# Second layer's expert stage: 56 rows ahead instead of 42, 14 of them parked in DRAM, eight rows' gates kept on chip, and gate products tied to the low half of W two rows back

## The chip, the cores and the metric

The kernel runs on one core of a Trainium2 chip. The metric is the time of one execution on the device in microseconds, as the median of three runs. One further execution was taken by the hardware profiler; all rows below come from it.

## The reference, cut to what matters

The reference is a two-layer block over 256 context tokens and 256 latent tokens of width 1024. Each layer has a mixer (a gated unit, a state space scan and gated linear attention) and then a feed-forward part that picks experts by product keys. The change lies in that second part:

```python
def block(xb):                                   # 128 tokens
    q = (xb @ w_query).reshape(128, 8, 2, 128)
    s = jnp.einsum('thpd,phkd->thpk', q, keys)   # 8 heads, two lists of 128 keys
    s1, i1 = lax.top_k(s[:, :, 0], 16);  s2, i2 = lax.top_k(s[:, :, 1], 16)
    cand = s1[..., :, None] + s2[..., None, :]   # 256 candidate pairs per head
    top_s, pos = lax.top_k(cand, 16)             # 16 experts of 128*128 per head
    gate = jax.nn.softmax(top_s, axis=-1)
    act = gelu(einsum('td,thkd->thk', xb, expert_u[idx]))
    return einsum('thk,thkd->td', gate * act, expert_v[idx])
```

The second layer gives out latent tokens only, so it works on two blocks of 128 tokens; the first layer works on four (one of them by gathering experts).

## The kernel before, in words

For most token blocks the kernel does not gather experts. It computes all 128 x 128 of them, row by row: row `e` holds the 128 experts whose first key is `e`. `U(e)` (lines 1324 to 1344) streams one 512 KB tile of expert_u, splits it into a high and a low half (`split`, lines 69 to 72: ScalarE casts `uhi`, VectorE subtracts `ulo`), has TensorE make the activations in `pu` (24 matrix products for two blocks, `mm3`, line 77) and lets ScalarE apply gelu into a tile that waits for its turn. `V(e)` (lines 1351 to 1375) streams a tile of expert_v, splits it in the same way (`vhi`, `vlo`), has VectorE multiply the activations by the gates (line 1362, "the gate product" below), splits the result into the two halves of W (`whl`: ScalarE casts the high one, line 1364, VectorE subtracts the low one, line 1365) and has TensorE add 12 products of 512 columns to the sums `acc` (line 1374).

The gates come from `gates`. For each group of 32 tokens VectorE builds one-hot matrices (`oh2`, `oh1l`, `oh1h`, `oh2s`, lines 1219 to 1227), TensorE multiplies them into `gps` (lines 1232, 1233), ScalarE copies them to `gst`, and a 2 MB write on ScalarE's queue stores them in DRAM (`gd`, line 1237). GpSimd copies the gates of rows 0 to 3 to `gt0` (line 1236); the gates of later rows are read back from DRAM four rows at a time into `gt` (line 1356), which has two buffers. In the second layer there are 8 groups and one `gt` is 512 KB.

The V rows need the gates, and the gates of all tokens. Until these are there TensorE works on U rows ahead of time: `LEAD` rows of them, 42 in the second layer. 16 of the 42 activations lie in four row buffers, the rest in `act` tiles. In the first layer `SPILL` rows are parked: their gelu goes to `aout` (two buffers), is written to DRAM on ScalarE's queue (line 1344) and read back into `ain` (three buffers, line 1349) two rows ahead of its use. After the rows ahead V rows run alone until U has to follow, and then U and V alternate, with U four rows ahead at the least (`KEEP`).

The order of the instructions on each engine is not the program's. A scheduler sets it when the kernel is built, from a timeline that it simulates; an engine then takes its instructions strictly in that order, so one that waits holds up all behind it on that engine. `self.after(...)` (line 55) makes the instructions that are traced inside it come behind a given one on the same engine. SyncE's queue issues all loads of `eraw` (five buffers), `gt` and `ain`, also in order.

Of the kernel before, what the change touches and what calls it, by code (L numbers as in the profile page):

```python
# [10 lines left out]
F32 = mybir.dt.float32  # L11
# [5 lines left out]
OP = mybir.AluOpType  # L17
# [11 lines left out]
PLAN = {"s5": ((4, 1, 0, 0, 0, 0), (4, 0, 0, 0, 0, 0)), "gla": ((1, 1, 1, 1, 0, 1, 1), (2, 2, 1, 1, 0, 1))}  # L29
DEPTH = 2  # L30
NI1 = 128
LEAD = {0: 40, 1: 42}
KEEP = 4
TOGETHER = {0: 4, 1: 3}
SPILL = {0: 22, 1: 0}
AHEAD = 2
ERAW = 5
GPS = 3
# [11 lines left out]
class Kernel:  # L50
# [1129 lines left out]
                self.topk_head(b, h, s, p)  # L1180


    def gates(self, l, blocks, p, ps):

        nc = self.nc
        gd = self.dp.tile([4 * len(blocks), 128, NI1 * 32], F32, name=f"gd{l}", bufs=1)
        sels = {}
        with self.pool(f"selx{l}", side="right") as sp:
            es = {b: self.pick_exp(b, sp, len(blocks)) for b in blocks}
            for b in blocks:  # L1190
                w = self.pick(b, sp, es[b])
                tb = ps.tile([128, 3, 128], F32, name="selp", tag="gps", bufs=GPS)
                for z in range(3):
                    nc.tensor.transpose(tb[:, z], w[:, z], self.ident)

                sels[b] = self.selp.tile([128, 4, 128, 2], F16, name=f"sel{b}", bufs=1)
                g = sp.tile([128, 2, 128], F32, name="gsel", bufs=2)
                nc.scalar.copy(sels[b][:, 0:2], tb[:, 0:2, :, None].to_broadcast([128, 2, 128, 2]))
                nc.scalar.mul(g[:, 0], tb[:, 2], 2.0 ** 14)
                nc.vector.tensor_copy(sels[b][:, 2], g[:, 0, :, None].to_broadcast([128, 128, 2]))  # L1200
                nc.vector.tensor_tensor(g[:, 1], g[:, 0], sels[b][:, 2, :, 0], op=OP.subtract)
                nc.vector.tensor_scalar(sels[b][:, 3], g[:, 1, :, None].to_broadcast([128, 128, 2]), 2.0 ** 12, None,
                                        op0=OP.mult)
        self.es_tv.close()

        self.gt0 = self.selp.tile([128, 4 * len(blocks), 4, 32], F32, name="gt0")
        with self.pool(f"gate{l}", side="right") as p:
            for k, b in enumerate(blocks):
                sel = sels[b]
                for tg in range(4):  # L1210
                    st = p.tile([128, NI1, 32], F32, name="gst", bufs=2)
                    for q in range(32 // OHT):
                        t = 32 * tg + OHT * q
                        ts = (128, OHT, 64, 2)
                        io = self.iota.rearrange("p (a b) -> p a b", b=2)[:, None].to_broadcast(ts)
                        at = lambda z: sel[:, z, t:t + OHT][:, :, None].to_broadcast(ts)
                        one = lambda nm: p.tile([128, OHT, 64, 2], F16, name=nm, bufs=OHB)
                        o2, o2s, oh, ol = one("oh2"), one("oh2s"), one("oh1h"), one("oh1l")
                        nc.vector.tensor_tensor(o2, io, at(1), op=OP.is_equal)
                        e = OSC[q % len(OSC)]  # L1220
                        if e == "a":
                            nc.scalar.mul(o2s, o2, 2.0 ** -12)
                        else:
                            nc.vector.tensor_scalar(o2s, o2, 2.0 ** -12, None, op0=OP.mult)
                        nc.vector.tensor_tensor(ol, io, at(0), op=OP.is_equal)
                        nc.vector.tensor_tensor(oh, ol, at(2), op=OP.mult)
                        nc.vector.tensor_tensor(ol, ol, at(3), op=OP.mult)
                        flat = lambda a, z: a[:, z].rearrange("p a b -> p (a b)")
                        for z0 in range(0, OHT, 4):
                            pb = ps.tile([128, 4, 128], F32, name="gps", tag="gps", bufs=GPS)  # L1230
                            for z in range(4):
                                nc.tensor.matmul(pb[:, z, :], flat(o2, z0 + z), flat(oh, z0 + z), start=True, stop=False)  # L1232
                                nc.tensor.matmul(pb[:, z, :], flat(o2s, z0 + z), flat(ol, z0 + z), start=False, stop=True)  # L1233
                            o = OHT * q + z0
                            nc.scalar.mul(st[:, :, o:o + 4], pb.rearrange("p t i -> p i t"), 2.0 ** -14)
                    nc.gpsimd.tensor_copy(self.gt0[:, 4 * k + tg], st[:, 0:4, :])
                    nc.scalar.dma_start(gd[4 * k + tg], st.rearrange("p i t -> p (i t)"))
        return gd

# [53 lines left out]
    def peer(self, l, dense):  # L1293
        nc, i = self.nc, self.i
# [5 lines left out]
        with ExitStack() as es:  # L1300
            p = es.enter_context(self.pool(f"peer{l}"))
            acts_a = es.enter_context(self.pool(f"acta{l}"))
            es_b = es.enter_context(ExitStack())
            acts_b = es_b.enter_context(self.pool(f"actb{l}"))
            lead, spill = LEAD[l], SPILL[l]
            per, away = 1024 // nt, {}
            pu_ = es.enter_context(self.pool(f"psu{l}", space=PSUM))
            with self.pool(f"psg{l}", space=PSUM) as gp:
                gd = self.gates(l, dense, p, gp)
            pa = es.enter_context(self.pool(f"psa{l}", space=PSUM))  # L1310
            p2 = es.enter_context(self.pool(f"peerv{l}", side="right"))
            acc = [[pa.tile([128, 512], F32, name=f"acc{b}{h}", bufs=1) for h in range(2)] for b in range(nb)]
            acts, gt, rows, todo, left = {}, {}, {}, [], []

            def stream(src, nm):
                raw = p.tile([128, 1024], F32, name="eraw", bufs=ERAW)
# [7 lines left out]
            def U(e):  # L1324
# [10 lines left out]
                elif e < 4 * per + spill:  # L1335
                    acts[e] = p.tile([128, nt], F32, name="aout", bufs=2)
                elif e < lead - KEEP:
                    acts[e] = acts_b.tile([128, nt], F32, name="act", bufs=lead - KEEP - 4 * per - spill)
                else:
# [9 lines left out]
                    nc.sync.dma_start(acts[e], away[e])  # L1349

            def V(e):
                if e == 0:
                    gt[0] = self.gt0
                elif e % 4 == 0:
                    gt[0] = p2.tile([128, 4 * nb, 4, 32], F32, name="gt", bufs=2)
                    nc.sync.dma_start(gt[0].rearrange("p g a b -> p g (a b)"),
                                      gd.rearrange("g p x -> p g x")[:, :, 32 * e:32 * e + 128])
# [1 line left out]
                hi, lo = stream(i["v"][l, e], "u" if late < TOGETHER[l] and late % 2 else "v")  # L1359
                a = acts.pop(e)  # L1360
                av = a.rearrange("p (g t) -> p g t", t=32)
                nc.vector.tensor_tensor(av, av, gt[0][:, :, e % 4, :], op=OP.mult)
                w = p2.tile([128, 2, nt], F32R, name="whl", bufs=max(3, TOGETHER[l]))
                nc.scalar.copy(w[:, 0], a)  # L1364
                self.v_lo = nc.vector.tensor_tensor(w[:, 1], a, w[:, 0].bitcast(F32), op=OP.subtract)
                todo.append((e, hi, lo, w))
                if 0 < late < TOGETHER[l]:
                    return
# [69 lines left out]
            for k, b in enumerate(sorted(out)):  # L1438
# [3 lines left out]
                st = ep.tile([128, 2], F32, name="fst", bufs=2) if last else self.xst[:, b]  # L1442
# [10 lines left out]
                else:  # L1453
                    nc.vector.tensor_tensor(st[:, 0:1], st[:, 0:1], st[:, 1:2], op=OP.add)
                    self.rstd(st[:, 1:2], st[:, 0:1], 1024)
                    if k == 0:
                        fg = ep.tile([128, 1024], F32, name="fg", bufs=1)
                        f = i["final_g"]
# [122 lines left out]
```

## Time and profile before

| | us |
|---|---|
| median of three runs | 2751.05 |
| lowest, highest | 2743.09, 2753.84 |
| profiled execution | 2751.38 |
| its span, first to last instruction | 2749.6 |
| TensorE busy | 2627.0 (96%) |
| VectorE busy | 2037.9 (74%) |
| ScalarE busy | 1188.9 (43%) |
| GpSimd busy | 430.6 (16%) |

The span holds both layers one after the other; the second layer's U rows begin near 1930 us, its gates end near 2116 us. TensorE's busy time counts pipelined products, so its rate is better read from how far apart products start. The 1.8 us between the span and the execution's time lie around it.

### The profile page before, as it was taken

What the parts mean: (1) busy time and instruction counts of PE and PEld (TensorE: products, weight loads), DVE (VectorE), ACT (ScalarE), POOL (GpSimd) and SP (SyncE); (2) the same over time, 40 slices, a digit from 0 to 9 for tenths busy, and PEclk for the clock granted to TensorE, in tenths of its full rate; (3) what the DMA queues carried; (4) which work ended last, traced back from release to release, by engine and by line L of the source; (5) the groups of instructions that cost most, each with busy time, mean ns of one, the idle gap of its engine ahead of it and who ended that gap; (6) DMA issues with size and microseconds to landing.
All of it is one profiled execution on the core that took longest, in us unless ns stands there. A gap on an engine that the chain in (4) does not pass through costs nothing.

```text
span 2749.6 us, 44156 instructions
## 1 busy us (share of the span) xinstructions
PE 2627.0 (96%) x16911; PEld 2272.0 (83%) x16911; DVE 2037.9 (74%) x4342; ACT 1188.9 (43%) x1808; POOL 430.6 (16%) x342
## 2 busy tenths in 40 slices
PE   7899999999899999999999999998897999999998
PEld 4777888899678899988899977768796789999997
DVE  8755589899788988988978755558998655555554
ACT  3353334566234333333333333524475454444443
POOL 0001000021023443434534200010011000000000
PEclk9998999999999999999999999989998999999999
DMA  7521423577689999999999837444566766666663
GB/s 275 135 86 63 169 84 116 203 292 290 207 282 330 335 332 344 326 333 345 327 343 334 319 119 203 135 158 165 184 242 249 252 211 211 207 207 208 211 210 115
DMA packets 250035, 629.59 MB, mean 229 GB/s; under 512 B 25376, under 2 KB 117856, under 8 KB 247008
## 3 DMA queue, kind: packets, MB, share of 16 engines
q1 hardware_dynamic: 197072, 432.41, 47.0%
q0 software_dynamic: 36864, 134.23, 13.6%
q10 hardware_dynamic: 15888, 60.14, 6.1%
q8 instruction: 132, 2.16, 0.3%
q14 instruction: 79, 0.65, 0.1%
HBM read 566.04 MB, written 59.61 MB: 228 GB/s over the span
## 4 chain that ended last, share of the span: by engine, by line
PE 82%; DVE 11%; DMA 3%; issue 2%; ACT 1%; POOL 0%; SPq 0%; POOLq 0%; DVEq 0%; ACTq 0%
PE pu L77 32%; PE acc L1374 31%; PE prT L275 6%; PE prN L288 3%; PE opp L941 1%; PE modp L157 1%; DMA mraw<-in_w_mod_dram 1%; PE gps L1233 1%; PE gps L1232 1%; DMA gt<-gd 1%; PE yp L633 1%; DVE wlo L72 1%; DVE ulo L72 1%; DVE ti L1092 1%; DVE s L1090 1%
## 5 line engine op out<-in xcount | busy, mean ns | idle before, releaser
L1374 PE MATMUL acc<-vhi,whl 128*128 128x512 f32 x2528 | 726.9, 398 | 3.2 <-ACT whl L1364 3.2
L77 PE MATMUL pu<-hTh,uhi 128*128 128x384 f32 (+1 forms) x2048 | 604.2, 313 | 11.3 <-ACT s L1176 7.5
L77 PE MATMUL pu<-hTl,uhi 128*128 128x384 f32 (+1 forms) x2048 | 603.0, 313 | 0.0
L1374 PEld LDWEIGHTS acc<-vhi,whl 128*128 128x128 f32 x2528 | 471.5, 190 | 107.1 <-ACT whl L1364 3.5
L72 DVE TENSOR_TENSOR vlo<-eraw,vhi 128x1024 fp32r<-128x1024 f32 x253 | 309.4, 1223 | 288.3 <-ACT vhi L71 286.3
L71 ACT CAST vhi<-eraw 128x1024 fp32r<-128x1024 f32 x253 | 266.1, 1052 | 530.5 <-PE acc L1374 508.7
L1374 PE MATMUL acc<-vlo,whl 128*128 128x512 f32 x1264 | 403.0, 400 | 23.3 <-DVE vlo L72 23.3
L77 PEld LDWEIGHTS pu<-hTh,uhi 128*128 128x128 f32 x2048 | 392.0, 191 | 23.1 <-ACT s L1176 7.7
L77 PEld LDWEIGHTS pu<-hTl,uhi 128*128 128x128 f32 x2048 | 392.1, 191 | 7.4
L71 ACT CAST uhi<-eraw 128x1024 fp32r<-128x1024 f32 x259 | 272.4, 1052 | 272.7 <-PE pu L77 254.4
L72 DVE TENSOR_TENSOR ulo<-eraw,uhi 128x1024 fp32r<-128x1024 f32 x259 | 316.8, 1223 | 91.8 <-ACT uhi L71 71.1
L77 PE MATMUL pu<-hTh,ulo 128*128 128x384 f32 (+1 forms) x2048 | 351.9, 311 | 0.0
L77 PEld LDWEIGHTS pu<-hTh,ulo 128*128 128x128 f32 x2048 | 313.4, 190 | 2.9 <-DVE po L1102 0.8
L1374 PEld LDWEIGHTS acc<-vlo,whl 128*128 128x128 f32 x1264 | 239.1, 190 | 83.0 <-DVE vlo L72 26.7
L1265 POOL DMA_INDIRECT grow<-in_v_dram,gidx x128 | 177.9, 1390 | 247.5 <-DVE gacc L1278 186.9
L1265 POOL DMA_INDIRECT grow<-in_un_dram,gidx x128 | 151.3, 1182 | 275.2 <-DVE grow L1271 156.1
L72 DVE TENSOR_TENSOR wlo<-raw,whi 128x1024 fp32r<-128x1024 f32 x84 | 102.5, 1221 | 113.1 <-ACT whi L71 112.4
L1278 DVE SCALAR_TENSOR_TENSOR gacc<-grow,gact,gacc 128x1024 f32<-128x1024 f32 x127 | 162.5, 1280 | 6.7 <-DMA grow<-in_v_dram,gidx 6.5
L1271 DVE SCALAR_TENSOR_TENSOR grow<-grow,h2n 128x1024 f32<-128x1024 f32 x128 | 155.6, 1217 | 5.3 <-DMA grow<-in_un_dram,gidx 5.3
L275 PE MATMUL prT<-hTl,whi 128*128 128x512 f32 (+1 forms) x448 | 156.9, 352 | 0.0
L275 PE MATMUL prT<-hTh,wlo 128*128 128x512 f32 (+1 forms) x448 | 154.6, 350 | 1.8 <-DVE wlo L72 1.8
L275 PE MATMUL prT<-hTh,whi 128*128 128x512 f32 (+1 forms) x448 | 156.1, 354 | 0.0
(416 smaller groups left out, 3746.0 us busy)
## 6 DMA issues: line engine op xcount, KB each, us to landing
eraw<-in_ut_dram SPq DMA_DIRECT2D x256, 512.0 KB
eraw<-in_v_dram SPq DMA_DIRECT2D x256, 512.0 KB
gd<-gst ACTq DMA_DIRECT2D x20, 2048.0 KB
mraw<-in_w_mod_dram SPq DMA_DIRECT2D x64, 512.0 KB
gt<-gd SPq DMA_DIRECT2D x31, 768.0 KB
raw<-in_w_in_dram SPq DMA_DIRECT2D x36, 512.0 KB
raw<-in_w_query_dram SPq DMA_DIRECT2D x32, 512.0 KB
eraw<-in_w_mod_dram SPq DMA_DIRECT2D x32, 512.0 KB
```

The source lines that it names most:

```text
L71: (hi_eng or nc.scalar.copy)(hi, src)
L72: self.last_lo = (lo_eng or nc.vector).tensor_tensor(lo, src, hi.bitcast(F32), op=OP.subtract)
L77: self.nc.tensor.matmul(out, a, b, start=n == 0, stop=n == len(ops) - 1)
L157: self.nc.tensor.matmul(acc[32 * kc:32 * kc + 32, :], self.sc[:, 4 * half + kc, :], raw[:, o:o + 512], start=half == 0 or not whole, stop= ...
L275: self.nc.tensor.matmul(bs[g], a[:, k, gs], b, start=z == 0 and k == 0 and q == 0, stop=z == 1 and k == 3 and q == 2)
L288: self.nc.tensor.matmul(o, a, b[:, k], start=z == 0 and k == 0 and q == 0, stop=z == 1 and k == 3 and q == 2)
L633: nc.tensor.matmul(bb[odd][:, gg, :], hin[hf, z, d, g // 2, :], rhs, start=n == 0, stop=False)
L941: mm = nc.tensor.matmul(ob[64 * k:64 * k + 64, cs], a, r, start=z == 0, stop=z == len(ops) - 1, tile_position=tp)
L1265: nc.gpsimd.indirect_dma_start(out=r, out_offset=None, in_=src, in_offset=bass.IndirectOffsetOnAxis(ap=idx[:, j:j + 1], axis=0))
L1271: v.scalar_tensor_tensor(r, r, 1.0, self.h2n, op0=OP.mult, op1=OP.mult, accum_out=act[:, j:j + 1])
L1278: v.scalar_tensor_tensor(acc, r, act[:, j:j + 1], acc, op0=OP.mult, op1=OP.add)
L1374: nc.tensor.matmul(acc[b][h], w[:, wk, bs], r[:, 512 * h:512 * h + 512], start=e_ == 0 and z == 0, stop=e_ == NI1 - 1 and z == 2)
```

## The change

Tables of numbers and one ordering rule are changed. In the second layer `LEAD` goes from 42 to 56 and `SPILL` from 0 to 14, so U rows 0 to 15 still lie in row buffers, rows 16 to 29 are parked in DRAM, and as many rows as before (22, and `KEEP` + 1) lie in `act` tiles. A new table `HOLD` sets how many rows' gates are kept on chip: 4 in the first layer as before, 8 in the second, whose GpSimd copies grow from 128 x 128 to 128 x 256 elements, and the first read of `gt` is then for row 8. In both layers the gate product of row `e` is ordered on VectorE behind the low half of W of row `e - 2`.

```diff
-LEAD = {0: 40, 1: 42}
+LEAD = {0: 40, 1: 56}
 KEEP = 4
+HOLD = {0: 4, 1: 8}
-SPILL = {0: 22, 1: 0}
+SPILL = {0: 22, 1: 14}
...
-        self.gt0 = self.selp.tile([128, 4 * len(blocks), 4, 32], F32, name="gt0")
+        self.gt0 = es.enter_context(self.pool(f"gt0_{l}", side="right")).tile([128, 4 * len(blocks), HOLD[l], 32], F32, name="gt0")
...
-                    nc.gpsimd.tensor_copy(self.gt0[:, 4 * k + tg], st[:, 0:4, :])
+                    nc.gpsimd.tensor_copy(self.gt0[:, 4 * k + tg], st[:, 0:HOLD[l], :])
...
-                if e == 0:
-                    gt[0] = self.gt0
+                if e < HOLD[l]:
+                    gt[0] = self.gt0[:, :, e - e % 4:e - e % 4 + 4]
...
-                nc.vector.tensor_tensor(av, av, gt[0][:, :, e % 4, :], op=OP.mult)
+
+                with self.after(*los[max(e - 2, 0):max(e - 1, 0)]):
+                    nc.vector.tensor_tensor(av, av, gt[0][:, :, e % 4, :], op=OP.mult)
...
                 self.v_lo = nc.vector.tensor_tensor(w[:, 1], a, w[:, 0].bitcast(F32), op=OP.subtract)
+                los.append(self.v_lo)
```

VectorE before, where the second layer's V rows begin, right behind the last one-hot matrix (`actr`, `act`: activations; `gt0`: gates on chip; `gt`: gates read from DRAM; `vlo`: low half of the expert_v tile; numbers tell tiles apart):

```order
L1362 TENSOR_TENSOR actr_19954<-actr_19954,gt0_18955 128x256 x4
L1365 TENSOR_TENSOR whl_21358<-actr_19954,whl_21358 128x256
L1365 TENSOR_TENSOR whl_21380<-actr_19954,whl_21380 128x256
L1365 TENSOR_TENSOR whl_21402<-actr_19954,whl_21402 128x256
L1362 TENSOR_TENSOR actr_20094<-actr_20094,gt_21439 128x256 x4
L1362 TENSOR_TENSOR actr_20239<-actr_20239,gt_21529 128x256 x4
L72 TENSOR_TENSOR vlo_21398<-eraw_21395,vhi_21397 128x1024
L1362 TENSOR_TENSOR actr_20379<-actr_20379,gt_21619 128x256 x3
L1365 TENSOR_TENSOR whl_21424<-actr_19954,whl_21424 128x256
```

Eight gate products of rows 4 to 11, which need two reads of `gt`, stand ahead of the `vlo` of row 2, and those of rows 12 to 14 ahead of the low half of W of row 3.

The same place of VectorE's order in the changed kernel:

```order
L73 TENSOR_TENSOR ulo_21818<-eraw_21815,uhi_21817 128x1024
L1365 TENSOR_TENSOR actr_19961<-actr_19961,gt0_18962 128x256 x2
L1368 TENSOR_TENSOR whl_21855<-actr_19961,whl_21855 128x256
L1365 TENSOR_TENSOR actr_19961<-actr_19961,gt0_18962 128x256
L1368 TENSOR_TENSOR whl_21877<-actr_19961,whl_21877 128x256
L1365 TENSOR_TENSOR actr_19961<-actr_19961,gt0_18962 128x256
L1368 TENSOR_TENSOR whl_21899<-actr_19961,whl_21899 128x256
L1365 TENSOR_TENSOR actr_20101<-actr_20101,gt0_18962 128x256
L73 TENSOR_TENSOR vlo_21895<-eraw_21892,vhi_21894 128x1024
L1368 TENSOR_TENSOR whl_21921<-actr_19961,whl_21921 128x256
L1365 TENSOR_TENSOR actr_20101<-actr_20101,gt0_18962 128x256
```

Only products with gates from `gt0` stand ahead of the `vlo` of row 2, and from there on one `vlo`, one low half of W and one gate product follow each other.

ScalarE before, at the end of the second layer's gates (`gst`: gates from PSUM; `gd`: their write to DRAM; `whl`: first high halves of W):

```order
L1222 ACTIVATE oh2s<-oh_19793 128x1024
L1235 ACTIVATE gst<-gps 128x128x4 x3
L1237 DMA gd_18829<-gst 128x4096
L1222 ACTIVATE oh2s<-oh_19851 128x1024
L1235 ACTIVATE gst<-gps 128x128x4 x8
L1237 DMA gd_18829<-gst 128x4096
L1364 CAST whl<-actr 128x256 x3
```

There the U rows are over and only gates are left.

ScalarE in the changed kernel, among the parked rows of the second layer (`aout`: the activations of a row to be parked; `act_24` and so on: their places in DRAM):

```order
L1236 ACTIVATE gst<-gps 128x128x4 x2
L1238 DMA gd_18833<-gst 128x4096
L72 CAST uhi<-eraw 128x1024
L1342 ACTIVATE aout<-pu 128x256
L1223 ACTIVATE oh2s<-oh_19144 128x1024
L1345 DMA act_24_20813<-aout 128x256
L72 CAST uhi<-eraw 128x1024
L1342 ACTIVATE aout<-pu 128x256
L1345 DMA act_25_20848<-aout 128x256
L1236 ACTIVATE gst<-gps 128x128x4 x3
```

Each parked row brings a cast, a gelu and the issue of a write; two writes of `gd` stand among the 14 parked rows, ahead of row 24 and of row 28.

SyncE before, at the start of the second layer's V rows (`eraw`: an expert tile; `fg`, `xe`: loads for the end of the kernel):

```order
L1317 DMA eraw<-in_v_dram 128x1024 x7
L1356 DMA gt<-gd_18829 128x8x128 x2
L1459 DMA fg<-in_final_g_dram 128x1024
L1356 DMA gt<-gd_18829 128x8x128 x2
L1317 DMA eraw<-in_v_dram 128x1024
L1441 DMA xe_27084<-xscr_15749 128x1024
L1356 DMA gt<-gd_18829 128x8x128 x2
```

SyncE in the changed kernel, some rows later, where the parked rows come back (`ain`: a parked row, `act_19` being row 19):

```order
L1357 DMA gt<-gd_18833 128x8x128
L1318 DMA eraw<-in_v_dram 128x1024 x3
L1350 DMA ain<-act_19_20638 128x256
L1318 DMA eraw<-in_v_dram 128x1024
L1350 DMA ain<-act_20_20673 128x256
L1357 DMA gt<-gd_18833 128x8x128
L1318 DMA eraw<-in_v_dram 128x1024
L1350 DMA ain<-act_21_20708 128x256
L1318 DMA eraw<-in_v_dram 128x1024
```

Before, the reads of `gt` crowd at the start of the V rows; now one follows after every fourth row, and between rows 19 and 29 each row also has its `ain`.

## Rows read from the trace of the kernel before

**Rows 1.** Windows: stretch, length; busy us (instructions) per engine; clock; DMA; GB/s.
```profile
1990.00:2086.70 96.70, 96.70 (x961) 95.04 (x959) 89.64 (x133) 67.06 (x105) 13.10 (x5) 1.00 0.70 251
2086.70:2115.70 29.00, 17.92 (x194) 15.75 (x192) 26.84 (x48) 18.98 (x31) 8.25 (x4) 0.82 0.52 218
2115.70:2150.10 34.40, 24.07 (x88) 17.87 (x88) 21.68 (x49) 10.66 (x17) 0.00 (x0) 0.85 0.92 300
```

**Rows 2.** Chain of waits, second layer's first V rows: start, us, what.
```profile
2122.17 5.84 DMA gt<-gd
...
2142.29 5.87 DMA gt<-gd
...
2150.13 80.86 PE acc L1374 x344
```

**Rows 3.** VectorE's timeline there: start, us, line, operation, tiles, count [idle before].
```profile
2112.85 0.69 DVE L1227 TENSOR_TENSOR oh1l<-oh1l,sel 128x1024 f16<-128x1024 f16 x1
...
2126.26 1.43 DVE L1362 TENSOR_TENSOR actr<-actr,gt 128x256 f32<-128x256 f32 x4 [8.17 <-DMA gt<-gd]
```

**Rows 4.** Chain of waits where U and V alternate: one U row, one V row.
```profile
2262.06 2.87 PE pu L77 x24
2264.93 2.80 PE acc L1374 x12
```

**Rows 5.** TensorE's timeline among the second layer's gates, first and last of 14.
```profile
2090.53 0.22 PE L1233 MATMUL gps<-oh1l,oh2s 128*128 128x128 f16 x1 [0.37 <-DVE oh1l L1227]
...
2091.26 0.22 PE L1233 MATMUL gps<-oh1l,oh2s 128*128 128x128 f16 x1
```

**Rows 6.** Groups by shape, 1990 to 2150 us: count, busy us, mean ns, idle before.
```profile
L72 DVE TENSOR_TENSOR ulo<-eraw,uhi 128x1024 fp32r<-128x1024 f32 x25 | 30.6, 1223 | 4.6 <-ACT uhi L71 3.5 <-issue 1.1
L1362 DVE TENSOR_TENSOR actr<-actr,gt 128x256 f32<-128x256 f32 x16 | 5.8, 420 | 11.7 <-DMA gt<-gd 9.6 <-POOL gt L1236 2.1
L1365 DVE TENSOR_TENSOR whl<-actr,whl 128x256 fp32r<-128x256 f32 x8 | 3.2, 419 | 0.0
...
L71 ACT CAST uhi<-eraw 128x1024 fp32r<-128x1024 f32 x24 | 25.1, 1048 | 16.8 <-PE pu L77 13.8 <-ACT act L1341 1.5 <-ACT oh2s L1222 1.0
L1341 ACT ACTIVATE act<-pu 128x256 f32<-128x256 f32 x26 | 10.0, 384 | 5.1 <-PE pu L77 4.9
L1364 ACT CAST whl<-actr 128x256 fp32r<-128x256 f32 x10 | 3.9, 402 | 4.1 <-DVE actr L1362 4.1
```

**Rows 7.** GpSimd's timeline, last two copies to gt0 in the second layer.
```profile
2106.10 6.87 POOL L1236 COPY gt<-gst 128x128 f32<-128x128 f32 x1 [9.28 <-ACT gst L1235]
2115.33 0.30 POOL L1236 COPY gt<-gst 128x128 f32<-128x128 f32 x1 [2.35 <-ACT gst L1235]
```

**Rows 8.** First layer: parked rows (ns min/median/max; idle before), then a gates' write.
```profile
L1344 ACTq DMA_DIRECT2D act<-aout x22: 326/326/331, 499.2 to 626.1; - x22
...
  PE pu L77: 2.9, 9
...
694.07 10.03 DMA gd<-gst
```

**Rows 9.** First layer: a parked row's read and its gate product; all waits (us, times).
```profile
758.76 0.34 SPq L1349 DMA_DIRECT2D ain<-act  x1
...
764.17 0.56 DVE L1362 TENSOR_TENSOR ain<-ain,gt 128x384 f32<-128x384 f32 x1 [1.33 <-DMA ain<-act]
...
  DMA ain<-act: 3.0, 4
```

**Rows 10.** First layer's first V rows: three gate products, then windows as in Rows 1.
```profile
713.44 1.49 DVE L1362 TENSOR_TENSOR ain<-ain,gt 128x384 f32<-128x384 f32 x3
...
690.00:720.00 30.00, 19.22 (x95) 14.28 (x94) 17.16 (x62) 7.14 (x13) 0.30 (x1) 0.77 0.72 230
720.00:790.00 70.00, 70.00 (x300) 56.31 (x299) 65.79 (x247) 28.15 (x38) 2.35 (x3) 1.00 0.65 207
790.00:810.00 20.00, 15.39 (x62) 11.77 (x61) 12.84 (x21) 4.49 (x7) 7.78 (x7) 0.97 0.85 300
```

More of the change, by code (lines that the diff above doesn't have):

```diff
@@ L1180, in query, with gates @@
                 self.topk_head(b, h, s, p)
-    def gates(self, l, blocks, p, ps):
+    def gates(self, l, blocks, es, ps):
         nc = self.nc
@@ L1188, in gates @@
         with self.pool(f"selx{l}", side="right") as sp:
-            es = {b: self.pick_exp(b, sp, len(blocks)) for b in blocks}
+            exps = {b: self.pick_exp(b, sp, len(blocks)) for b in blocks}
             for b in blocks:
-                w = self.pick(b, sp, es[b])
+                w = self.pick(b, sp, exps[b])
                 tb = ps.tile([128, 3, 128], F32, name="selp", tag="gps", bufs=GPS)
@@ L1308, in peer @@
             with self.pool(f"psg{l}", space=PSUM) as gp:
-                gd = self.gates(l, dense, p, gp)
+                gd = self.gates(l, dense, es, gp)
             pa = es.enter_context(self.pool(f"psa{l}", space=PSUM))
@@ L1312, in peer @@
             acc = [[pa.tile([128, 512], F32, name=f"acc{b}{h}", bufs=1) for h in range(2)] for b in range(nb)]
-            acts, gt, rows, todo, left = {}, {}, {}, [], []
+            acts, gt, rows, todo, left, los = {}, {}, {}, [], [], []
             def stream(src, nm):
```

## Prediction, before the changed kernel ran

> **What bounds the kernel now.** I read the page's busy times first: TensorE is busy for 96% of the span, so the kernel is bound by TensorE wherever it is fed, and a change can gain only where TensorE stands still. The slices of the span then show where that is, and the windows around the second layer's first V rows [rows 1] give its size. Up to 2086.70 us, when the last of the 42 rows ahead ends, TensorE is busy 96.70 of 96.70 us. In the next 29.00 us it issues 194 gate products; fourteen of them start within 2091.26 - 2090.53 = 0.73 us when nothing holds them up [rows 5], 0.056 us each, so this stretch holds 194 x 0.056 = 10.9 us of work. The clock granted there is 0.82. In the 34.40 us after that, up to 2150.10, it issues 88 products of the V rows; a V row of 12 takes 2.80 us [rows 4], so they are worth 88 x 2.80 / 12 = 20.5 us, at a clock of 0.85. In all 29.00 + 34.40 - 10.9 - 20.5 = 32.0 us are lost in this place.
>
> Why they are lost is in the chain of waits [rows 2] and VectorE's timeline [rows 3]. First VectorE builds one-hot matrices alone (busy 26.84 of 29.00) while TensorE has no U row left; the last one starts at 2112.85. Then VectorE's next work is eight gate products with gates read back from DRAM, and they stand ahead of the `vlo` of row 2. The chain goes through four reads of `gt` (the first shown at 2122.17 with 5.84, the last at 2142.29 with 5.87), VectorE stands 8.17 us ahead of the products at 2126.26, and only at 2150.13 an unbroken piece of 344 V products begins.
>
> **The change part by part.** I start from the profiled execution, 2751.38 us (span 2749.6 and 1.8 around it); the median of the runs shown is 2751.05, so no correction is needed.
>
> *56 rows ahead.* The U and V rows of a layer stay 128 each; 14 U rows come ahead of the V rows instead of beside them. A U row is 2.87 us [rows 4], so 14 x 2.87 = 40.2 us of TensorE work stand ready for the stretch in which it stood still. With the 10.9 us of gate products TensorE is full until 2086.7 + 10.9 + 40.2 = 2137.8. If gates and first V rows are ready by then, all 32.0 us are gained. The later parts cost TensorE nothing: V rows alone run 50 instead of 36 rows, 12 products each as before, then U and V alternate at 2.87 + 2.80.
>
> Is VectorE ready? From 2086.70 it has 26.84 us up to the last one-hot matrix's end, less the first few products. To it come 14 `ulo` of 1.223 [rows 6] = 17.1, and two `vlo` that were made early (2.4) go behind: 41.5 us. In the mixed stretch before, it ran at 89.64 of 96.70, or 93% [rows 1]; 41.5 / 0.93 = 44.8, which is 2131.5, 6 us ahead of TensorE. ScalarE has 18.98 us and 14 x (1.048 + 0.384 + 0.326) = 24.6 more (cast, gelu [rows 6], issue of a write [rows 8]), less two `vhi`, 2.1: 41.5 us. It fits into 51 us if ScalarE is kept at 81%. In the mixed stretch it was at 67.06 of 96.70, 69%, with TensorE full; at that pace it would need 60 us and end at 2146.6. But it waited there mostly for TensorE to make `pu` (13.8 of the 16.8 us ahead of its casts [rows 6]), so 69% is what was asked of it. What may still be lost is bounded by 0 (none was lost in the mixed stretch) and 5 (half of the gap of 8.8, rounded up); near the first, I take +2.
>
> *Eight rows' gates on chip and the order of gate products.* Now only products that need no read stand ahead of `vlo` of row 2, and the first `gt` is needed by row 8, 8 x 2.80 = 22 us after V starts. A read takes 5.9 us [rows 2], so the four leave the chain; this part of the gain is in the 32.0. VectorE needs `vlo` 1.22, low W 0.42 and product 0.42 = 2.06 per V row of 2.80: it fits. What is late next is GpSimd's copy to `gt0`, now of twice the width. The last but one took 6.87 us among VectorE's work, the last 0.30 with VectorE idle [rows 7]. Bounds: 0, and, if the last one takes 2 x 6.87 = 13.7 from about 2129 (some 2.5 before VectorE is done), then product 0.42 and cast 0.40: 2143.5, 5.7 late. Since VectorE's last work before it are a few `ulo` and then the product that itself waits for the copy, I take 0.
>
> The Trainium skill, "SBUF — State Buffer", section "SBUF: two separate sides", says that VectorE and GpSimd share one pair of ports as a lock that is held for a whole instruction, so that the other one stands. The two copies of this trace agree (6.87 against 0.30). By that rule alone the upper bound of this step would hold, which is the third rival.
>
> *Parked rows, writing.* 14 writes of `aout`, 128 KB each, over two buffers. In the first layer 22 such writes show no wait ahead of them other than TensorE's `pu` [rows 8]; there a row is 192 KB. Lower bound 0. Upper: two of the 2 MB writes of `gd` now stand among the parks, each 10.03 us [rows 8]; a park behind one may be late by 10.03 less the two buffers' rows, 2 x 3.6 (a U row and its share of the gates, 51.1 / 14): 2.8, twice 5.7. I take 0, as in the first layer.
>
> *Parked rows, reading.* 14 reads of `ain` on SyncE's queue, past the loads of `eraw` and `gt`. In the first layer 22 of them cost VectorE 3.0 us of waiting in all, 4 times [rows 9]. Lower bound 0. Upper: `ain` has three buffers, so a read starts when the product and W of two rows earlier are done; VectorE's 2.06 and the 5.41 from issue to landing (758.76 to 764.17 [rows 9]) make 7.47 per two rows, 3.73 a row instead of 2.80, for the 11 rows 19 to 29 that 3 buffers can't take in advance: 10.3. In bytes it is tight: (512 + 128 + 128) KB per 2.80 us is 281 GB/s, and the most that this place shows is 300 at a DMA share of 0.92 [rows 1]. I take 3.0 / 22 x 14 = +2.
>
> *First layer.* Only the ordering rule applies. VectorE's first three products take 1.49 us [rows 10]; five that stood ahead of the `vlo` of row 2 go behind it, 5 x 0.50 = 2.5. The stretch 690 to 720 lost 30.00 - 19.22 = 10.8, with the read of `gt` behind a 10.03 us write in it, which stays. Bounds: all of it and of the 4.6 lost in 790 to 810 gained, or those 4.6 lost once more, since the gathering's first step there meets other neighbours. I take -2.5.
>
> Sum: -32.0 + 2 + 0 + 0 + 2 - 2.5 = -30.5, which is 2751.4 - 30.5 = **2721**. Own range 2712 (first layer gains all, nothing else lost) to 2729 (the bounds of two of the small terms).
>
> **The rivals.** *First: the reads pace VectorE.* The 10.3 in place of 2 makes 2729. For it: landing takes 5.41 us behind the `eraw` loads, and reads now come at 2.80 us a row instead of the first layer's 4.2 (1.5 times the blocks). Against it: from 720 to 790 TensorE was busy 70.00 of 70.00 with such reads in it [rows 10].
>
> *Second: ScalarE sets the pace of the gates.* It issues the parks behind `gd` writes, in order, so the casts behind them wait as well. With 8.8 instead of 2 the time is 2728, with the 5.7 of the writes on top 2733.5. For it: the 69% above; against it: that it waited for TensorE.
>
> *Third: GpSimd's doubled copy starts V 5.7 us late:* 2727. For it: 6.87 beside 0.30. Against it: VectorE has nothing left to hold the ports with.
>
> *Fourth, slower: the ordering rule makes V rows serial.* With product `e` behind low W of row `e - 2` VectorE cannot run ahead while it waits; if cast 1.05, `vlo` 1.22, cast of W 0.40, low W 0.42 and product 0.42 followed one another, a V row would take 3.51 instead of 2.80, and 50 rows alone 50 x 0.71 = 35.5 us more: 2756.5, with the reads' 10.3 on top 2767. It decides from 32.0 / 50 = 0.64 us a row, that is 3.44. Against it: in 720 to 790 the products already follow one per row in this order by themselves, and TensorE is full.
>
> That the change doesn't do what it says is no rival: the order shows 14 more U rows ahead of V and no read of `gt` ahead of row 8.
>
> **How the numbers follow.** The forecast has a chance of 0.68, the rivals in turn 0.14, 0.11, 0.03 and 0.04. This kernel can be told from no change from about 0.5%, so faster means below 2737.3 and slower above 2764.8. Forecast and first three rivals lie below 2737.3 unless several upper bounds come together, to which I give 0.08: faster 0.88. The fourth rival is split, 0.03 for slower with the reads on top, 0.01 for same: same 0.09. The range for 8 in 10 goes from 2710 (a first layer that gains more than the rule gives) to 2740 (second rival and reads together).
>
> **What would show it.** Right: in the second layer TensorE is full with a clock of 1.00 from 2086 on until the V rows begin near 2138 (some 2.5 earlier by the first layer's gain), no `gt` in the chain of waits there, no wait for `vlo` of several us, V rows at 2.80, waits for `ain` and `aout` of about 2 us in all. Wrong: TensorE waiting for ScalarE or VectorE among the gates (second rival), V rows of rows 19 to 29 at 3.7 with waits for `ain` (first), a copy of 10 us and more ahead of the first V row (third), V rows well above 2.80 outside the parked ones (fourth), or a first layer whose stretch 690 to 810 differs by over 5 us.

## The result, and the profile after

The changed kernel takes 2717.06 us (median of four runs, 2708.60 to 2721.47) against 2749.14 for the kernel before on the same chip (2743.09 to 2753.84): a ratio of 0.9875, 95% interval 0.9853 to 0.9898. The forecast was 2721. The profiled execution's span went from 2749.6 to 2718.0, 31.6 us less.

Windows of the changed kernel over the stretch of [rows 1]; the third goes up to where its V rows begin, the last through its parked rows; columns as there.

```profile
1990.00:2086.70 96.70, 96.70 (x971) 94.80 (x970) 91.27 (x134) 69.45 (x109) 11.99 (x5) 1.00 0.75 271
2086.70:2115.70 29.00, 29.00 (x301) 28.41 (x300) 27.38 (x41) 20.55 (x33) 1.86 (x2) 1.00 0.67 236
2115.70:2134.80 19.10, 18.35 (x175) 17.79 (x173) 12.10 (x17) 12.14 (x22) 0.40 (x1) 1.00 0.89 324
2134.80:2180.00 45.20, 45.18 (x193) 36.36 (x194) 30.23 (x50) 21.01 (x32) 0.00 (x0) 1.00 0.80 277
2180.00:2215.00 35.00, 32.45 (x138) 25.17 (x136) 20.70 (x33) 16.32 (x24) 0.00 (x0) 1.00 0.77 248
```

The 29.00 us in which TensorE issued 194 short products at a clock of 0.82 now hold 301 products of U rows and gates at 1.00, and ScalarE is busy 32.69 of 48.10 us up to the V rows, 68%, where the mixed stretch before had 69%. TensorE stands for 0.75 us just ahead of the V rows (third row) and for 2.55 us among the parked rows (last row). The 11 rows from 19 on take 3.11 us each on average, from first product to first product, instead of 2.81, but not evenly: rows 19, 23 and 27 take 3.32, 4.35 and 4.09 us, the others 2.81.

The chain of waits there (start, us, what), where [rows 2] had four reads of `gt`:

```profile
2129.33 4.73 PE pu L78 x39
2134.82 48.07 PE acc L1378 x204
2182.91 1.06 ACT vhi L72
2184.04 1.11 issue
2185.25 3.17 DMA eraw<-in_v_dram
2188.43 1.21 DVE vlo L73
```

U products run into V products, and 204 of these, 17 rows, pass unbroken, up to the first parked row. VectorE's timeline ahead of the first V row, as in [rows 3]:

```profile
2121.63 0.68 DVE L1228 TENSOR_TENSOR oh1l<-oh1l,sel 128x1024 f16<-128x1024 f16 x1
...
2130.47 0.76 DVE L1365 TENSOR_TENSOR actr<-actr,gt 128x256 f32<-128x256 f32 x2 [1.13 <-POOL gt L1237]
2134.80 0.42 DVE L1368 TENSOR_TENSOR whl<-actr,whl 128x256 fp32r<-128x256 f32 x1 [3.57 <-ACT whl L1367]
```

The longest and the last of GpSimd's eight copies of the second layer, as in [rows 7], and VectorE where the longest ends:

```profile
2014.54 4.59 POOL L1237 COPY gt<-gst 128x256 f32<-128x256 f32 x1 [159.33 <-ACT gst L1236]
...
2130.03 0.40 POOL L1237 COPY gt<-gst 128x256 f32<-128x256 f32 x1 [15.75 <-ACT gst L1236]
```

```profile
2018.18 0.69 DVE L1227 TENSOR_TENSOR oh1h<-oh1l,sel 128x1024 f16<-128x1024 f16 x1
2019.61 1.23 DVE L73 TENSOR_TENSOR ulo<-eraw,uhi 128x1024 fp32r<-128x1024 f32 x1 [0.73 <-ACT uhi L72]
```

VectorE has its first products 4.3 us before TensorE's first V product. The eight copies, twice as wide as before, took 0.40 to 4.59 us; the eight of the kernel before took 0.30 to 6.87. The longest ends at 2019.13, in a pause of VectorE that begins at 2018.87.

For the sums below, a stretch's loss is its length less its products by kind: 2.87 / 24 us for one of a U row, 2.81 / 12 for one of a V row of the second layer, 0.056 for one of the gates, each product counted where it starts. From 2087 to 2150 that is 31.9 us before (18.5 while the gates are built alone, 13.4 behind the reads) and 2.4 after; from 2175 to 2250 it is 3.3 us after and nothing before. The expectations below were written with 18.3 for the 18.5. The second layer from its first U product to its last V product took 805.9 us and takes 781.6; the first layer from first to last V product 939.5 and 935.0. What lies between the layers gave 2.8 us, and the second layer's first 100 us lost 1.5 more (17.3 instead of 15.9).

### The profile page after: what moved, and what is told of

Its sections match the earlier page's. It is cut to its first block, busy times and chain, and to the rows that moved or that the text cites. A ratio compares the mean times of both kernels' runs of the same rounds, so it can differ in the third digit from the quotient of the medians.

```text
span 2718.0 us, 44207 instructions
## 1 busy us (share of the span) xinstructions
PE 2613.1 (96%) x16911; PEld 2263.1 (83%) x16911; DVE 2038.0 (75%) x4342; ACT 1188.7 (44%) x1808; POOL 418.2 (15%) x342
## 3 DMA queue, kind: packets, MB, share of 16 engines
q0 software_dynamic: 36864, 134.23, 13.7%
## 5 line engine op out<-in xcount | busy, mean ns | idle before, releaser
L78 PE MATMUL pu<-hTh,uhi 128*128 128x384 f32 (+1 forms) x2048 | 605.3, 313 | 12.1 <-ACT s L1177 7.5
L1266 POOL DMA_INDIRECT grow<-in_v_dram,gidx x128 | 171.9, 1343 | 233.0 <-DVE gacc L1279 179.4
```

Source lines behind the costliest of these rows:

```text
L78: self.nc.tensor.matmul(out, a, b, start=n == 0, stop=n == len(ops) - 1)
L1266: nc.gpsimd.indirect_dma_start(out=r, out_offset=None, in_=src, in_offset=bass.IndirectOffsetOnAxis(ap=idx[:, j:j + 1], axis=0))
```

## The experiments

Each kernel was timed beside the kernel before on its chip. The stages are from one profiled execution each, first to last product as above, so they scatter: changed, rule_late, rule_early, gap24 and lead44 have the same settings in the second layer and show 778.6 to 783.6 us there, and the stretch between the two layers, which no run sets out to change, took 288.4 to 308.9 us. A difference of a few us between two entries says little by itself.

| kernel | median, us | ratio to before (95%) | first layer, us | second layer, us |
|---|---|---|---|---|
| before | | | 939.5 | 805.9 |
| changed | 2717.06 | 0.9875 (0.9853 to 0.9898) | 935.0 | 781.6 |
| rule_only | 2738.46 | 0.9956 (0.9942 to 0.9970) | 932.8 | 799.9 |
| lead_only | 2743.33 | 0.9966 (0.9950 to 0.9981) | 939.8 | 797.1 |
| no_rule | 2736.98 | 0.9951 (0.9934 to 0.9967) | 939.3 | 796.7 |
| hold4 | 2725.35 | 0.9907 (0.9891 to 0.9924) | 934.9 | 785.9 |
| lead49 | 2725.28 | 0.9904 (0.9882 to 0.9927) | 933.1 | 782.7 |
| lead60 | 2721.84 | 0.9892 (0.9874 to 0.9910) | 934.0 | 781.0 |
| ahead3 | 2718.06 | 0.9865 (0.9843 to 0.9887) | 936.2 | 776.8 |
| rule_late | 2727.87 | 0.9914 (0.9880 to 0.9948) | 938.8 | 782.0 |
| rule_early | 2720.51 | 0.9889 (0.9865 to 0.9913) | 933.9 | 778.6 |
| gap24 | 2724.48 | 0.9899 (0.9880 to 0.9917) | 938.2 | 781.5 |
| lead44 | 2712.68 | 0.9858 (0.9837 to 0.9880) | 908.9 | 783.6 |
| best44 | 2714.20 | 0.9858 (0.9833 to 0.9883) | 907.7 | 781.1 |

### The three parts, taken apart

**rule_only**, against the kernel before (only the ordering rule is in):

```diff
-LEAD = {0: 40, 1: 56}
+LEAD = {0: 40, 1: 42}
-HOLD = {0: 4, 1: 8}
+HOLD = {0: 4, 1: 4}
-SPILL = {0: 22, 1: 14}
+SPILL = {0: 22, 1: 0}
```

> The kernel before with the ordering rule alone in both layers (42 rows ahead, nothing parked in the second layer, four rows' gates kept). Theory A (each stretch is worth what the row counts say): the 18.3 us lost while gates are built alone stay; of the 13.4 us lost behind reads of gt one read stays ahead of the vlo of row 2 (about 7 us), so 6 us are gained there, and the first layer gains the 4.3 us by which its last V product came earlier in the changed kernel: about -10 us, 2739. Rival B (the first layer's 4.3 us are scatter of that one execution, not the rule): -6 us, 2743. Rival C (the rule makes V rows serial where more than one read is outstanding): no gain or slower, 2749 or more.

12.7 us faster than before (2751.17 there), where theory A said 10. The loss behind the reads fell from 13.4 to 7.0 us. That while the gates are built alone stayed: the first V product comes 185.9 us after the layer's first U product, as before. Windows, columns as above:

```profile
2087.00:2112.60 25.60, 16.19 (x169) 14.06 (x166) 23.33 (x41) 16.58 (x28) 15.56 (x3) 0.73 0.47 196
2112.60:2150.00 37.40, 33.25 (x130) 26.39 (x131) 20.01 (x34) 14.38 (x22) 0.00 (x0) 0.91 0.79 273
```

One of GpSimd's copies to `gt0`, 128 x 128 elements as before, stands in its chain of waits with 14.57 us:

```profile
2092.14 14.57 POOL gt L1237
```

**lead_only**, **no_rule** and **hold4**, against the changed kernel. In the first two the rule is off (a new constant, `RULE = ()`), lead_only and hold4 keep four rows' gates:

```diff
-HOLD = {0: 4, 1: 8}
+HOLD = {0: 4, 1: 4}
...
-                with self.after(*los[max(e - 2, 0):max(e - 1, 0)]):
+                with self.after(*(los[max(e - 2, 0):max(e - 1, 0)] if l in RULE else [])):
```

> 56 rows ahead with 14 parked, but four rows' gates kept and no ordering rule. Theory A: the 18.3 us are filled, but the products of rows 4 to 13, which need three reads of gt, stand ahead of the vlo of row 2 again, and the last write of gd is only over near 2139.5; third read landed near 2153, so row 2 is about 14 us late, and the first layer's 4.3 us are not gained: -31.6 + 14 + 4.3 = -13 us, 2736. Rival B (more rows ahead are the whole gain; the reads hide behind TensorE's U rows): -27 us or better, 2722. Rival C (late gates just move the hole): -5 us or less, 2744.

> The changed kernel without the ordering rule, with eight rows' gates kept. Theory A: keeping eight rows by itself buys nothing, since VectorE's order then puts the products of rows 8 to 18 with three reads of gt ahead of the vlo of row 2: about as lead_only, -13 us, 2736. Rival B (eight rows kept are what takes the reads off the path; the rule adds nothing in the second layer): -27 us, 2722, that is the changed kernel less the first layer's 4.3.

> The changed kernel with four rows' gates kept in the second layer. Theory A: one product (row 4) with a read of gt stands ahead of the vlo of row 2; the last write of gd is over near 2139.5, the read takes 5.9 us, so the vlo of row 2 ends near 2147 instead of 2140.2: 6 to 7 us slower than the changed kernel, -25 us against before, 2724. Rival B (the rule alone hides the reads, the kept gates buy nothing): as the changed kernel, -31.6 us, 2717. Rival C (the kept gates are half of the second layer's gain): -18 us, 2731.

no_rule and hold4 came out as theory A had them (2736.98 for 2736, 2725.35 for 2724); lead_only, at 2743.33, is nearer to C's 2744 than to A's 2736. What A said of the place holds there: 2.5 us are lost from 2087 to the first V product, and 12.9 behind the reads. The chain of no_rule shows why eight rows kept are worth nothing by themselves (two of the three reads stand in it):

```profile
2129.91 10.37 DMA gd<-gst
...
2140.36 4.19 DMA gt<-gd
...
2144.57 1.44 DVE actr L1366 x4
...
2146.03 4.36 DMA gt<-gd
...
2151.09 1.23 DVE vlo L74
2152.32 0.04 issue
2152.36 22.73 PE acc L1379 x87
```

The stretch before the V rows is as full as in the changed kernel (2.5 us lost), but VectorE has taken the products of rows 8 to 17 ahead of the `vlo` of row 2, and three reads of `gt` stand between row 1 and row 2: 13.1 us lost. In hold4 it is one read, for row 4:

```profile
2130.78 9.59 DMA gd<-gst
...
2140.43 4.27 DMA gt<-gd
...
2145.07 1.23 DVE vlo L73
2146.30 0.04 issue
2146.34 28.77 PE acc L1378 x116
```

There the loss is 5.5 us. What theory A did not have: without the rule the parked rows cost 7.3 us between 2175 and 2250 (lead_only and no_rule), with it 3.3 and 3.8 (changed kernel and hold4). That, with the 12.9 us behind the reads, leaves lead_only 8.8 us of gain in the second layer. By that layer's time, rows ahead alone give 8.8, the rule alone 6.0, both 20.0 and all three 24.3, each with the scatter named above.

### How many rows ahead

**lead49** and **lead60**, against the changed kernel (lead60: 60 and 18):

```diff
-LEAD = {0: 40, 1: 56}
+LEAD = {0: 40, 1: 49}
-SPILL = {0: 22, 1: 14}
+SPILL = {0: 22, 1: 7}
```

> The changed kernel with 49 rows ahead and 7 parked in the second layer: half of the added rows. Theory A (the stretch ends by whichever is later, TensorE's work or VectorE's gates plus splits of the rows ahead): with 42 rows the V rows began at 2112.6 with 16.1 us lost while gates were built alone; seven rows add 9 us of VectorE time to the gates and 20.1 us of TensorE work, so 5 us stay lost; fewer parked rows give back about 1: 4 us slower than the changed kernel, 2721. Rival B (the hole fills in proportion to the rows): 8 us lost, 2725. Rival C (the rows ahead cost the gates nothing): none lost, 2716 to 2717.

> The changed kernel with 60 rows ahead and 18 parked in the second layer. Theory A (at 56 rows the stretch is full: TensorE has U rows until 2134, VectorE is ready at 2130.5; more rows only move work from behind to ahead): the V rows begin 4 x 2.87 = 11.5 us later and end at the same time; first U product to last V product of the second layer 781.6 us as with 56 rows, plus 0.7 for four more parked reads; 2717 to 2718. Rival B (gates or ScalarE still set the start of the V rows at 56): 2 us or more gained, under 780. Rival C (each parked row read back costs VectorE more than two rows' cover): 784 or more, 2720.

Windows of lead49, then of lead60, to the first V product and beyond:

```profile
2087.00:2118.60 31.60, 25.89 (x276) 24.21 (x275) 27.93 (x44) 21.70 (x37) 6.92 (x3) 0.95 0.68 258
2118.60:2150.00 31.40, 31.40 (x134) 25.29 (x135) 21.00 (x36) 14.41 (x23) 0.00 (x0) 1.00 0.86 309
```

```profile
2087.00:2116.00 29.00, 29.00 (x296) 28.35 (x295) 27.93 (x42) 21.27 (x35) 3.92 (x2) 1.00 0.70 247
2116.00:2144.30 28.30, 28.30 (x269) 28.05 (x268) 19.82 (x27) 17.90 (x30) 2.42 (x2) 1.00 0.88 307
```

lead49 lost 8.8 us from 2087, and its median is 2725: rival B's forecast came out, not A's 5 us and 2721. A's base was wrong: with 42 rows the loss begins ahead of 2087 (4.3 us from 2030 to there in rule_only, against 1.8 in the changed kernel). From 2030 to the first V product it is 20.7 us with 42 rows, 10.6 with 49, 4.3 with 56 and 3.4 with 60. A's sum from 20.7 is 20.7 + 9 - 20.1 = 9.6 for 49 rows, and in proportion to the rows, between 42 and 56, it would be 12.5. The 10.6 lie between the two, so this run does not decide between A's mechanism and B's. Its seven parked rows lost nothing, 3.3 us less than the changed kernel's. lead60 has the second layer at 781.0, as A said: four rows more moved the first V product from 2134.8 to 2144.3 and brought no gain that can be told from the scatter. Its median, 4.8 us above the changed kernel's, has an overlapping interval.

### The parked reads

**ahead3**, against the changed kernel:

```diff
-AHEAD = 2
+AHEAD = {0: 2, 1: 3}
-SPILL = {0: 22, 1: 14}
+SPILL = {0: 22, 1: 15}
```

> The changed kernel with the parked rows of the second layer read three rows ahead instead of two (four ain buffers instead of three; for the room one more row is parked, 15). Theory A (a read is issued when the buffer comes free, two rows' time is about what it takes to land, and the 13.1 us that VectorE waits for them cost TensorE 2.3 us between 2180 and 2215): those waits fall to under 4 us and TensorE's loss to under 0.5: -2 us against the changed kernel, 2715. Rival B (the bytes per row are the limit, 281 GB/s asked): waits and loss stay, 2717.

The second layer's parked reads in the changed kernel, from issue to landing, and waits in the parked rows (us in total, times, longest):

```profile
DMA to landing us min/median/max: 3.0/4.0/5.5
```

```profile
DVE ain L1365 <- DMA ain<-act: 13.1, 9, 2.9
PE acc L1378 <- DVE vlo L73: 2.5, 3, 1.3
```

The landings are not alike. SyncE's queue, the landing of the `ain` shown, and VectorE behind it:

```profile
2193.71 0.37 SPq L1357 DMA_DIRECT2D gt<-gd  x1
2194.85 0.33 SPq L1318 DMA_DIRECT2D eraw<-in_v_dram  x1
2195.28 0.37 SPq L1350 DMA_DIRECT2D ain<-act  x1
```

```profile
2195.28 5.47 DMA ain<-act
```

```profile
2200.84 0.42 DVE L1365 TENSOR_TENSOR ain<-ain,gt 128x256 f32<-128x256 f32 x1 [2.90 <-DMA ain<-act]
2201.18 1.22 DVE L73 TENSOR_TENSOR vlo<-eraw,vhi 128x1024 fp32r<-128x1024 f32 x1
```

Three of the 11 reads are the first behind a read of `gt` in the queue, and they land after 5.0 to 5.5 us; five land after 3.0 to 3.4, the other three after 4.0 to 5.0. For the three VectorE's gate product waits longest (2.52, 2.90 and 2.40 us), a `vlo` that TensorE needs stands behind that product, and these are TensorE's three waits. In lead60, with 15 such reads, TensorE's long rows are 19, 23, 27 and 31, again every fourth, as the reads of `gt` come.

In ahead3 the whole list of VectorE's waits there, and a window of its parked rows:

```profile
DVE vlo L73 <- ACT vhi L72: 16.2, 18, 0.9
```

```profile
2200.00:2235.00 35.00, 35.00 (x151) 28.11 (x151) 23.20 (x38) 17.50 (x26) 0.00 (x0) 1.00 0.84 275
```

The waits for `ain` are gone and TensorE is full, at 275 GB/s, with the reads of `gt` in the same queue: one row more of cover was enough, and the bytes were not the limit. The median, 2718.06, does not show it; its interval holds the changed kernel's ratio.

### The first layer

**rule_late** and **rule_early** (`e >= 16` and `e < 16`) keep the rule in the first layer for some rows; **gap24** has none there and puts the gathered experts' first step off:

```diff
-                with self.after(*los[max(e - 2, 0):max(e - 1, 0)]):
+                with self.after(*(los[max(e - 2, 0):max(e - 1, 0)] if l == 1 or e >= 16 else [])):
```

```diff
+RULE = (1,)
...
-        yield 10
+        yield 24
```

> The changed kernel, with the ordering rule in the first layer only from row 16 on (second layer whole). It asks where the first layer's 4 us come from, read from the last V product of that layer: 1635.5 to 1636.6 without the rule, 1631.2 to 1631.5 with it. Theory A: not at the first V rows but near 800 us, where before two products of rows 30 and 31 wait 3.63 us for gates from DRAM ahead of a vlo; those go behind it here: last V product near 1632, time as the changed kernel, 2717 to 2718. Rival B (the prediction's step: the five products ahead of the vlo of row 2): the gain is gone, last V product near 1635 to 1636, 2721. Rival C (the gathered experts' first step comes two rows later): gone as well, since that step stands here as before the change.

> The changed kernel, with the ordering rule in the first layer only up to row 15. Here the gathered experts' first step stands as late as in the changed kernel, and the products of rows 30 and 31 stand ahead of a vlo again. Theory A (those two products are the gain): last V product near 1635, time 2721. Rival B (the five products at the first V rows): last V product 1631 to 1633, 2717 to 2719. Rival C (the gathered experts' first step): the same as B, told apart from it by the stretch 705 to 720, in which B has TensorE some 10 products further.

> The changed kernel without the ordering rule in the first layer, but with the gathered experts' first step there put off by some rows by its own due time (24 units instead of 10), so that it stands two rows later on VectorE, as the rule had moved it; the products of rows 30 and 31 stand ahead of a vlo as before. After rule_late and rule_early: Theory A (VectorE used to reach the first gathered rows before they had landed and kept a vlo behind them; two rows later they have landed): from the first to the last V product of the first layer 935 us, as with the whole rule (932.8 to 936.2), not 939 (938.8 to 939.8); TensorE loses about 1 us instead of 3.3 to 5.2 around the first gathered rows. Rival B (the rule's order at the first V rows is what counts, and the gathered step is a sign of it): 939, loss unchanged. Rival C (the two products of rows 30 and 31 cost the most): 938, loss about 4.

Theory A of the first pair fell: rule_late, with the products of rows 30 and 31 behind, has 938.8 us from first to last V product, no better than without the rule, and rule_early, with them ahead, 933.9. Theory A of gap24 fell too: 938.2, not 935. C's numbers came out (938, 4.1 us lost around the first gathered rows), but rule_early has the same two products ahead and lost 0.9 there. VectorE's first steps with gathered rows and its longer waits there, before, then in the changed kernel, then in gap24:

```profile
793.52 1.23 DVE L1271 SCALAR_TENSOR_TENSOR grow<-grow,h2n 128x1024 f32<-128x1024 f32 x1 [4.41 <-DMA grow<-in_un_dram,gidx]
...
803.22 1.03 DVE L1362 TENSOR_TENSOR act<-act,gt 128x384 f32<-128x384 f32 x2 [3.63 <-DMA gt<-gd]
```

```profile
800.16 1.23 DVE L1272 SCALAR_TENSOR_TENSOR grow<-grow,h2n 128x1024 f32<-128x1024 f32 x1 [3.56 <-DMA grow<-in_un_dram,gidx]
```

```profile
800.32 1.23 DVE L1273 SCALAR_TENSOR_TENSOR grow<-grow,h2n 128x1024 f32<-128x1024 f32 x1 [2.25 <-DMA grow<-in_un_dram,gidx]
...
810.27 0.56 DVE L1366 TENSOR_TENSOR ain<-ain,gt 128x384 f32<-128x384 f32 x1 [2.52 <-DMA ain<-act]
```

In gap24 the later step lost less, and a wait for a parked row came up behind it. What the kernels do settle is where the gain lies. The five that lack the rule at the first layer's first V rows (before, lead_only, no_rule, rule_late, gap24) need 938.2 to 939.8 us, mean 939.1; the seven that have it with 40 rows ahead 932.8 to 936.2, mean 934.3. Of these 4.8 us, counted by products (a V row of this layer has 18), 1.6 are in the 60 us from the first V product (13.7 lost without, 12.1 with, on average) and 3.4 around the first gathered rows, 92 to 124 us after it (5.1 and 1.7). Which instruction there pays is open: ahead3 has the changed kernel's order of VectorE in this layer and lost 3.9 us there instead of 1.6; when transfers land may be the reason, which is not shown.

### The same remedy in the first layer

**lead44**, against the changed kernel; **best44** has the change of ahead3 besides:

```diff
-LEAD = {0: 40, 1: 56}
+LEAD = {0: 44, 1: 56}
-SPILL = {0: 22, 1: 14}
+SPILL = {0: 26, 1: 14}
```

> The changed kernel with 44 rows ahead and 26 parked in the first layer instead of 40 and 22: the same remedy in the other layer. The first layer loses about 11 to 12 us between its first V product and the vlo of row 2, and 4.7 more while the last gates are built. Theory A (the hole is there because no U row is left; four rows are 4 x 4.0 = 16.0 us of TensorE work, and VectorE gets 4 x 1.22 = 4.9 us more ahead of the vlo of row 2): the loss after the first V product falls to 3 or less, the four more parked rows cost under 1: -8 to -10 us against the changed kernel, 2708. Rival B (the vlo of row 2 stands behind the sorting of the gathered block, which waits for a transfer behind the last gates and is put off with the V rows): the hole stays 8 or more, 2715.

> The changed kernel with both: 44 rows ahead and 26 parked in the first layer, and in the second the parked rows read three rows ahead (15 parked). Theory A: the two gains add, as they lie in different layers: -10 to -12 us against the changed kernel, 2706, with VectorE waiting under 4 us for ain in the second layer. Rival B (only the first layer's counts, since the 2 us of the reads come back elsewhere): as lead44.

The windows of lead44 that answer to [rows 10]:

```profile
690.00:720.00 30.00, 26.32 (x174) 23.12 (x173) 15.39 (x42) 11.78 (x19) 0.29 (x1) 1.00 0.81 263
720.00:790.00 70.00, 70.00 (x301) 56.27 (x300) 68.85 (x264) 27.21 (x37) 0.00 (x0) 1.00 0.69 224
```

The hole behind the first V product is gone (nothing lost in its first 60 us, where the changed kernel loses 12.9), which is theory A's place. But V began 21.7 us later for 16.0 us of work, 4.4 us were lost 60 to 92 us after it, and the layer's last V product came at 1626.8 instead of 1631.2: 4.4 us, half of A's price. lead44 at 2712.68 and best44 at 2714.20 are the lowest medians here, and their intervals overlap that of the changed kernel: a version better than the changed one is likely and not shown.

## Why the prediction was right, step by step

- *56 rows ahead, -32.0.* Right in place and size: 31.9 us were there by the products, 2.4 are left. The clock of [rows 1], 0.82 and 0.85, is 1.00 throughout.
- *Coupling among the gates, +2.* 2.4. ScalarE kept its 68% with TensorE full, so the second rival, that this is its own limit, did not come; and lead60, with four more rows of TensorE's work, gained nothing that can be told from the scatter, so no other engine is seen to set the V rows' start at 56 rows.
- *Gates kept and the order of products.* The reads left the chain, as said. The prediction had priced the two as one. They are not equal. At the first V rows the eight rows bring nothing without the rule (13.1 us lost behind the reads in no_rule, 12.9 in lead_only) and 5.5 us with it (none in the changed kernel, 5.5 in hold4). The rule brings 13.1 there, and 4.0 more at the parked rows (7.3 to 3.3).
- *GpSimd's wider copy, 0.* Right, and for the reason given, that VectorE has nothing left to do there: the last copy took 0.40 us, and VectorE waited 1.13. The third rival's copy of 13.7 us did not come at this place. But the price of a copy was misread from two of eight [rows 7]: it does not go by the width. The other six of the kernel before took 4.50, 0.98, 6.83, 0.64, 0.64 and 0.59 us, also among VectorE's work. Each copy of over 2 us in the second layer of the kernel before and of the changed kernel ended 0.15 us (old width) or 0.26 us (new), to within 0.01, after VectorE's next pause began, however short it was. And a copy of the third rival's length did occur, at half the width: 14.57 us in rule_only, while VectorE went from one one-hot matrix to the next without a pause. Why that copy could end when it did, and why those of 0.6 to 0.8 us among VectorE's work needed no pause, the rows do not show. The lock that the Trainium skill describes ("SBUF — State Buffer", section "SBUF: two separate sides") is not refuted by these copies; the long ones, which end with a pause, agree with it. The long copy cost rule_only nothing that shows, since its first V product came 185.9 us after the first U product, as before.
- *Parked writes, 0.* Right: in the second layer TensorE and VectorE show no wait for them; one wait of 1.5 us fell on a cast of ScalarE.
- *Parked reads, +2.* 3.3 us, and not by the step's reasoning. It scaled VectorE's waits of the first layer to 1.9 us; they are 13.1, so the "about 2 us in all" that the prediction wanted to see for `ain` was wrong. The first rival's mechanism, a read that starts only when a buffer comes free, is there, but at three reads and not at every row. With a landing of 3.0 to 3.4 us, (2.06 + 3.4) / 2 = 2.73 us a row fits into 2.81. With the 5.0 to 5.5 us behind a read of `gt`, up to (2.06 + 5.5) / 2 = 3.78, it does not. ahead3, with one buffer more, has none of these waits.
- *First layer, -2.5.* The term that was mis-sized: 4.3 to 4.8 us, inside its bounds. The named cause, five products fewer ahead of the `vlo` of row 2, is worth 1.6 at the most (the kernel before lost 12.5 us in those 60 us, the changed kernel 12.9). The greater part lies at the gathered rows, which the prediction held for a bound only.
- *The fourth rival.* V rows outside the parked ones go at 2.81 us: the rule made nothing serial.

By the steps: -29.5 in the hole, +3.3 for the reads and -4.3 in the first layer make -30.5; what lies between the layers (-2.8), the second layer's first rows (+1.5) and small remainders bring the spans' 31.6. That the three make the forecast's own -30.5 is luck: the reads cost 1.3 more than forecast, the hole kept 0.5 more, and the first layer gave 1.8 more, for the most part at another place than the one named. The hole, nine tenths of the gain, was right by its mechanism.

## What to carry to other kernels

A hole in the bounding engine is worth its length less the work that is there in it: count products by kind, start the count where the rate first falls, and fill it with work that is due anyway up to where the other engines are ready. On an engine that takes its instructions in order, early work that may have to wait belongs behind the work that the bound waits for; keeping more data on chip brought almost nothing until the order used it. For a ring of buffers, compare use plus landing, divided by the rows read ahead, with the time of one row, and take the landing of the read that stands behind the largest other read in its queue: at the median of 4.0 us the excess looks even over the rows, and it lay in three of them.

## What was not expected of the hardware

The time of a copy on GpSimd did not go by its width: 0.30 to 14.57 us for 128 x 128 elements in the second layer of the kernel before and of rule_only, 0.40 to 4.59 for 128 x 256 in that of the changed kernel, and in the kernel before and the changed one those of over 2 us ended with VectorE's next pause. The same instruction order of VectorE lost 1.6 us in one execution and 3.9 in another around the first gathered rows. With TensorE fed by gates alone, the granted clock was 0.73 in rule_only and 0.82 before; with U rows among them it was 1.00.
